# Streaming encoder layer on one core: projections opened behind the head norms, longer planned waits for chain and norms, splits behind the third quarter of value rows

## The chip, the cores and the metric

The kernel runs on one core of a Trainium2 chip. The metric is the device time of one execution in microseconds, as the median of several runs. The profile is of one further execution; times inside it count from its first instruction.

## What is computed

One layer for 576 frames (64 of a running stream, 512 of a new one) of width 1024, all in fp32. The part that the change touches is the time mixing, in 16 heads of 64, and the value rows of the gated MLP:

```python
h = rms_norm(x, g_pre_mix); p = h @ w_in            # r|k|v|lora, u, value rows, two gates
xm = p + (p_prev - p) * mu_shift                    # token shift, for r, k, v and the lora columns
kk = k * k_k; kk = kk / max(norm_per_head(kk), 1e-12)
for t: sa = S @ a_t                                 # a = -kk, b = kk * a_rate
       S = S * w_t + sa b_t^T + v_t k_t^T;  y_t = S @ r_t
o_a = (group_norm(y) + bonus) * g
o_b = u * (tril(W_s) @ layer_norm(value rows) + b)
m = sigmoid(gate_a) * (o_a @ w_proj_a) + sigmoid(gate_b) * (o_b @ w_proj_b)
x = x + rms_norm(m @ w_o);  x = x + rms_norm(swiglu(rms_norm(x)))
```

## The kernel before

Every large product is made of three fp32r matmuls (high by high, high by low, low by high part). A weight block of 128 columns is loaded by SP (`wraw`, line 295), its high part is made on ACT (`whi`, line 302) and the low part on POOL in two instructions of 512 columns (`wlo`, line 305). One such projection block (`project`) is 48 matmuls `pj` of 288 columns, two halves of the frames of 8 x 3 each.

The 16 heads are worked as 8 pairs (128 rows). The recurrence over frames is cut into chunks of 64. For each pair `elementwise` makes the decays and the head norm (matmuls `n` over the squares `q`, wait `n2`), then the chunk scores (matmuls `am` over `AR` and `BK`, wait `am0`), and signals `A`; after a bonus term it signals `elem`. `turns` transposes keys and values and signals `tb` and `values`. `inverse` inverts the chunk's triangular matrices: a recurrence of 15 steps on DVE (`Xt`, `X`, lines 862 and 865, two instructions a step), then small matmuls with copies; it signals `it`, and handles one pair after the other. `batch` (matmuls `d`, `e`, `c`, `y`) signals `inv`. `chain` carries the state over the 9 chunks: matmuls `pc` into one bank, then DVE adds `S` or `So` from that bank (line 1004); its first step has two chunks, six more follow with a planned wait `S` after each, then the output rows `py`. It starts the wait `ch0` after `inv`. `finish` makes the group norm (a POOL power `gm`, line 1035), turns the result and writes `d_oa`.

TensorE's order is written out at build time by a planner, the class `Weave`. It keeps a clock in microseconds that each matmul advances, runs the streams above as generators, and lets each go on when a planned wait (a number of the table `LAT`, with a key such as `n2@0` for pair 0 alone) or an event has passed; between them it puts the matmuls of the projection blocks, which are a queue of items. An item can be taken when its `need` event is there; `load_next` takes the first that can, two blocks ahead of its matmuls. The items are `k`, `r`, `v` of the next pair with a need, and fillers (gates and `u`, evacuated as `st`, lines 430 and 432) without one; behind the last pair come four quarters of value rows (`gv_quarter`, matmuls `gv` of 256 columns, 5 x 24 a quarter) and then the products `pa`, `pb` and so on (`behind`). A `k`, `r` or `v` block is evacuated (`shc` first, line 484) only after the pair before has signalled `elem`. Banks of PSUM are counted too: `ps1(name, hold)` books one of four for `hold` microseconds, and `clk.free(n)` waits until n are free.

The other engines' order is not written out by the planner; the framework's schedule sets it when the program is built, and each engine then works its queue in that order.

`oa_all` comes when the last pair's chain has ended: it loads the time-mix results of seven pairs, waits `oa`, and splits each into high and low part (`cut`: ACT and DVE, wait `oaj` between), loads `bias` and `wsT` after the fourth, and signals `mp`, for which `pa` waits.

Of the kernel before, what the change touches and what calls it, by code (L numbers as in the profile page):

```python
# [12 lines left out]
P = 128  # L13
# [23 lines left out]
FILL = (2, 2, 2, 2, 2, 2, 2, 6)  # L37
LAT = {
# [4 lines left out]

# [1 line left out]
}  # L45


# [186 lines left out]
def layer(tc, I, O):  # L234
# [4 lines left out]
    f = lambda t: t.bitcast(F32)  # L239

    def mk(name, **kw):
        es = ExitStack()
        return es, es.enter_context(tc.tile_pool(name=name, bufs=1, **kw))
# [18 lines left out]
    def ps1(name, hold=0.0):  # L262
        clk.take(hold)
        return psum.tile([P, 512], F32, tag="a", bufs=nb["a"], name=name)
# [5 lines left out]
    clk = Weave()  # L270

    def mmul(out, lhsT, rhs, **kw):
        n = 1
        for d in rhs.shape[1:]:
            n *= d
        rows = lhsT.shape[0]
        if rows != clk.rows:
            clk.now += 0.12
            clk.rows = rows
        if rhs.dtype == F32R:  # L280
            clk.now += 0.011 + n / 2400
        elif rows == P:
            clk.now += max(n, P) / 600
        else:
            clk.now += n / 2000 if rows == 64 else 0.037 if rows == 32 else 0.02
        return pe.matmul(out, lhsT, rhs, **kw)  # L286
# [46 lines left out]
    def mm(outs, wb, xh, xl, k, kts, halves=(0, 1), cut=HALF):  # L333

        hi, lo = wb[k // KD]
        ws = slice((k % KD) * P, (k % KD + 1) * P)
        for n, (w, x) in enumerate(((hi, xh), (hi, xl), (lo, xh))):
            for h in halves:
                mmul(outs[h], w[:, ws], x[k][:, h * cut:(cut, T)[h]], start=k == 0 and n == 0, stop=k == kts - 1 and n == 2)
# [52 lines left out]
    def item(need, srcs, body):  # L392
        return (need, lambda: [wraw(src) for src in srcs], lambda raws, pin=True: [wsplit(r, pin=pin) for r in raws], body)

    def project(blk, done, need=None, after=()):

        def body(ws):
            held = []
            for h in range(2):
                ps = psd("pj")[:, 0:HALF]  # L400
                for k in range(KD):
                    mm({h: ps}, ws, hh, hl, k, KD, halves=(h,))
                    yield
                held.append((h, ps))
                while h == 1 and any(ev not in clk.events for ev in after):
                    yield True
                while held and all(ev in clk.events for ev in after):
                    done(*held.pop(0))
        return item(need, [I["w_in"][blk]], body)

    def shift_block(name, base, p_):
        take = []

        def done(h, ps):
            if h == 0:
                take.append(Shifted(base + p_, name))
            EV[p_][name] = take[0](h, ps)
            if h == 1:
                clk.signal(name, p_)
        after = [("elem", p_ - 1)] + [("values", p_ - 1)] * (name == "v") if p_ > 0 else []  # L420
        return project(base + p_, done, need=("A", p_ - 1) if p_ > 0 else None, after=after)

    def spill(base, j, dst, need=None):
        st = []
# [72 lines left out]
    for k in range(KD):  # L497
        t = xp.tile([P, T], F32, name=f"x{k}")
# [46 lines left out]
    with tc.manual_schedule(engines={mybir.EngineType.PE}):  # L545
        pk = [psd("pk")[:, 0:HALF]]
        rb = [psd("rb"), ps1("rb")]
# [52 lines left out]
    for k in range(KD):  # L600
        t = xp.tile([P, T], F32, tag="xsq", bufs=4, name="xn")
# [15 lines left out]
    S = fixed("S", NCH + 1, HD)  # L617
# [34 lines left out]
    def elementwise(E):  # L652
        hp_ = E["hp"]
# [40 lines left out]
        for j in range(5):  # L694
            mmul(s[:, j, :], q2[:, START2[j]:START2[j] + P], bones[:, 0:P:64], start=True, stop=True)
        clk.now += LAT["n2t"]
        rn = rp.tile([P, 10], F32, tag="rn", bufs=2, name="rn")
        dve.tensor_scalar(rn, s.rearrange("p j h -> p (j h)"), 1e-24, None, ALU.max)
        dve.reciprocal(rn, rn)
# [27 lines left out]
        E["AB"] = AB  # L727
        maskb = mask.unsqueeze(1).broadcast_to([P, 4, P])
        inner = lambda pm, rows_, rows, x, c: mmul(pm[rows_].rearrange("p (a t) -> p a t", t=64), BK[rows, x, c * 64:(c + 1) * 64], AR[rows, :, c * 64:(c + 1) * 64], start=True, stop=True)
        banks = lambda: [ps1("am", 3.6).rearrange("p (j t) -> p j t", t=P) for _ in range(2)]  # L730
        yield from clk.free(4)
        pm = banks()
        for c, j, half_ in PLACES2[:8]:
# [374 lines left out]
    def keepers(xs, pair):  # L1108
        xs[0].append(pair[0])
        xs[1].append(pair[1])  # L1110

    def mixed(name, **kw):
        return R["mp"].tile([P, T], F32, tag=name, name=name, **{"bufs": 1, **kw})

    def oa_all():

        yield (("chain", NPAIR - 1), 0.0)
        r_es.close()
        R["m"], R["mp"] = mk("merge")
        raw = []  # L1120
        wide = lambda n: R["mp"].tile([P, D], F32, tag=n, bufs=1, name=n)

        def load(j):
            raw.append(wide(("bias", "wsT")[j - 2])[:, 0:T] if j in (2, 3) else mixed(("gin", "", "zb", "xt")[j // 2], bufs=2))
            sp.dma_start(raw[j], d_oa[j])

        def cut(j):
            keepers(oas, split(R["mp"], raw[j], f"m{j}", eng=(dve, pool)[OAE[j]]))

        for j in range(NPAIR - 1):  # L1130
            load(j)
        yield LAT["oa"]
        for j in range(NPAIR - 1):
            cut(j)
            if j == 3:
                R["bias"], R["wsT"] = wide("bias"), wide("wsT")
                sp.dma_start(R["bias"], I["rows"][2:3, :].broadcast_to([P, D]))
                sp.dma_start(R["wsT"].rearrange("p (g t) -> p g t", t=P), I["wsT"])
            yield LAT["oaj"]
        clk.signal("mp")  # L1140
        yield (("oa", NPAIR - 1), 0.0)
        load(NPAIR - 1)
        yield LAT["oa"]
        cut(NPAIR - 1)
        yield (("behind",), 0.0)
        r2_es.close()
        l_es.close()
        h_es.close()
        R["d0"], R["dp0"] = mk("hidden0", side="right")
        R["x"], R["xf"] = mk("xf", side="right")  # L1150
        R["f"], R["fp"] = mk("ffnin", side="right")
        R["m2"], R["map"] = mk("merge2")
        clk.signal("xf")
# [151 lines left out]
    y, xt = [], []  # L1305
# [233 lines left out]
```

## Time and profile before

| | us |
|---|---|
| median of 3 runs | 1239.83 (1239.71 to 1240.45) |
| profiled execution | 1237.7 |
| its span, first to last instruction | 1235.9 |
| of it 60 to 541.4 (pair loop): TensorE busy | 461.01 of 481.40 |
| of it 541.4 to 618.7 (value rows): TensorE busy | 73.72 of 77.30 |
| TensorE busy in all | 1187.6 |

PE is TensorE's matmuls, PEld its weight loads, DVE, ACT and POOL the vector, scalar and GpSimd engines, SP the engine that issues the DMAs. Matmuls overlap, so the step from one start to the next tells their rate and not the length of one. The granted clock stands as a share of the full 2.4 GHz.

### The profile page before, as it was taken

How to read it: one execution, taken by the hardware profiler on the slowest of the kernel's cores; microseconds unless marked ns; L12 is line 12 of the kernel's file. 1: busy time of each engine (PE TensorE's matmuls, PEld its weight loads, DVE VectorE, ACT ScalarE, POOL GpSimd, SP SyncE). 2: the span in 40 equal slices, each digit the busy share in tenths (PEclk: the TensorE clock that was granted, in tenths of full speed). 3: DMA queues.
4: the chain of work that ended last, by engine and by line, in shares of the span. 5: the costliest groups of instructions: out<-in, count | busy, mean ns of one | idle time of the engine just before them, and what ended most of it. 6: DMA issues, size and time to landing. Idle time of an engine off the chain costs nothing.

```text
span 1235.9 us, 29949 instructions
## 1 busy us (share of the span) xinstructions
PE 1187.6 (96%) x12926; PEld 1154.5 (93%) x12926; DVE 547.8 (44%) x1081; ACT 466.1 (38%) x889; POOL 614.1 (50%) x484
## 2 busy tenths in 40 slices
PE   7989999989999989899899999899999999999997
PEld 6989898889899989899899999899999999999996
DVE  5756556665555565632624431654333333300003
ACT  5555544443545434333431233442222222222220
POOL 6665354635354545333445553566565555634442
PEclk9999999998999999999999999899999999999998
DMA  5233222222222222231554542232222222252222
GB/s 184 81 106 90 72 82 85 73 70 67 72 82 85 82 63 72 79 97 63 174 173 129 181 141 86 69 128 85 74 82 86 86 86 85 69 168 83 78 77 77
DMA packets 68276, 118.05 MB, mean 96 GB/s; under 512 B 30832, under 2 KB 36208, under 8 KB 68144
## 3 DMA queue, kind: packets, MB, share of 16 engines
q1 hardware_dynamic: 68000, 116.06, 30.9%
q8 instruction: 101, 1.65, 0.6%
q14 instruction: 31, 0.25, 0.1%
q10 hardware_dynamic: 144, 0.08, 0.0%
HBM read 99.83 MB, written 16.28 MB: 94 GB/s over the span
## 4 chain that ended last, share of the span: by engine, by line
PE 76%; DVE 13%; ACT 3%; issue 3%; POOL 3%; DMA 2%; SPq 0%; DVEq 0%; POOLq 0%; ACTq 0%
PE fg L286 20%; PE pj L286 16%; PE po L286 15%; PE pb L286 4%; PE gv L286 4%; PE pa L286 3%; POOL wlo L305 2%; DVE X L865 2%; DVE Xt L862 2%; PE am L286 2%; PE z L286 1%; PE d L286 1%; DVE TD L965 1%; PE pc L286 1%; DVE y L1324 1%
## 5 line engine op out<-in xcount | busy, mean ns | idle before, releaser
L305 POOL TENSOR_TENSOR wlo<-raw,whi 128x512 fp32r<-128x512 f32 (+1 forms) x288 | 400.5, 1413 | 374.2 <-ACT whi L302 344.3
L302 ACT ACTIVATE whi<-raw 128x1024 fp32r<-128x1024 f32 x144 | 149.7, 1046 | 279.6 <-PE fg L286 174.6
L1290 DVE TENSOR_TENSOR rs<-rs,nsq 128x288 f32<-128x288 f32 (+2 forms) x12 | 9.0, 754 | 105.9 <-ACT nsq L1289 105.9
L1358 DVE TENSOR_TENSOR ft<-ft,fg 128x288 f32<-128x288 f32 x40 | 16.4, 451 | 68.0 <-PE fg L286 66.5
L1352 DVE TENSOR_TENSOR fg<-fg,rs 128x288 f32<-128x288 f32 x40 | 16.5, 453 | 63.2 <-PE fg L286 63.1
L1355 DVE SCALAR_TENSOR_TENSOR ft<-ft,fg 128x576 f32<-128x576 f32 (+1 forms) x24 | 28.7, 1197 | 19.0 <-ACT ft L1354 19.0
L1356 POOL TENSOR_TENSOR ft<-ft,rs 128x576 f32<-128x576 f32 (+1 forms) x24 | 31.8, 1327 | 7.1 <-DVE ft L1355 7.1
L286 PE MATMUL pc<-S,TD 128*128 128x64 f32 x112 | 20.9, 270 | 13.1 <-DVE So L1004 10.8
L286 PEld LDWEIGHTS pc<-S,TD 128*128 128x128 f32 x112 | 18.3, 198 | 15.6 <-DVE So L1004 12.2
L865 DVE TENSOR_TENSOR X<-X,Xt 80x15 f32<-80x15 f32 (+7 forms) x120 | 29.4, 245 | 3.9
L862 DVE TENSOR_TENSOR Xt<-X,M 80x15 f32<-80x15 f32 (+7 forms) x120 | 29.3, 245 | 3.6
L1035 POOL TENSOR_TENSOR gm<-gm,mhalf 128x10 f32<-128x10 f32 x8 | 16.2, 2022 | 27.3 <-DVE gm L1034 27.2
L1004 DVE TENSOR_TENSOR S<-pc,C 128x64 f32<-128x64 f32 x48 | 10.5, 219 | 42.8 <-PE pc L286 42.8
L286 PE MATMUL pj<-h5h,whi 128*128 128x288 f32 x88 | 28.4, 323 | 0.0
L765 POOL TENSOR_TENSOR BK<-BK,EL 128x576 f32<-128x576 f32 x16 | 19.8, 1238 | 16.9 <-PE am L286 16.9
L286 PE MATMUL pj<-h0h,whi 128*128 128x288 f32 x88 | 28.2, 320 | 0.0
L286 PE MATMUL pj<-h6h,whi 128*128 128x288 f32 x88 | 28.1, 320 | 0.0
L286 PE MATMUL pj<-h3h,whi 128*128 128x288 f32 x88 | 27.9, 317 | 0.0
L286 PE MATMUL pj<-h7h,whi 128*128 128x288 f32 x88 | 27.7, 315 | 0.0
L286 PE MATMUL pj<-h1h,whi 128*128 128x288 f32 x88 | 27.6, 314 | 0.0
L286 PE MATMUL pj<-h2h,whi 128*128 128x288 f32 x88 | 27.6, 314 | 0.0
L286 PE MATMUL pj<-h4h,whi 128*128 128x288 f32 x88 | 27.6, 313 | 0.0
(1200 smaller groups left out, 4281.4 us busy)
## 6 DMA issues: line engine op xcount, KB each, us to landing
raw<-in_w_in SPq DMA_DIRECT2D x50, 512.0 KB, 3.7
raw<-in_w_gate SPq DMA_DIRECT2D x22, 512.0 KB, 3.7
raw<-in_w_up SPq DMA_DIRECT2D x22, 512.0 KB, 3.6
raw<-in_w_down SPq DMA_DIRECT2D x16, 512.0 KB, 3.5
raw<-in_w_gv SPq DMA_DIRECT2D x8, 512.0 KB, 3.6
raw<-in_w_proj_a SPq DMA_DIRECT2D x8, 512.0 KB, 3.8
raw<-in_w_proj_b SPq DMA_DIRECT2D x8, 512.0 KB, 3.7
raw<-in_w_o SPq DMA_DIRECT2D x8, 512.0 KB, 3.7
```

The source lines that it names most:

```text
L286: return pe.matmul(out, lhsT, rhs, **kw)
L302: keep(act.activation(hi[:, :cols], raw[:, :cols], ACT.Copy))
L305: keep(pool.tensor_tensor(lo[:, c0:c1], raw[:, c0:c1], f(hi[:, c0:c1]), ALU.subtract))
L765: pool.tensor_tensor(by_chunk(BK[:, x, :]), by_chunk(BK[:, x, :]), EL[:, :, 64:65].broadcast_to([P, NCH, 64]), ALU.mult)
L862: ins = dve.tensor_tensor(t3, X[:, 0:r, s:s + 1].broadcast_to([NU, r, w]), M[:, s:s + 1, s + 1:SB].broadcast_to([NU, r, w]), ALU.mult)
L865: dve.tensor_tensor(X[:, 0:r, s + 1:SB], X[:, 0:r, s + 1:SB], t3, ALU.add)
L965: dve.tensor_tensor(TD[rows, cs, rows], ps[rows, :, 1, :], by_place[rows, cs, 0, :], ALU.add)
L1035: pool.tensor_tensor(m, m, mhalf, ALU.pow)
L1352: keep(dve.tensor_tensor(g[:, HS[h]], pg, rs2[:, HS[h]], ALU.mult))
L1355: keep(dve.scalar_tensor_tensor(t[:, ts], t[:, ts], 1.0, g[:, ts], ALU.add, ALU.mult))
L1356: pool.tensor_tensor(t[:, ts], t[:, ts], rs2[:, ts], ALU.mult)
L1358: dve.tensor_tensor(t[:, HS[h]], t[:, HS[h]], pu, ALU.mult)
```

## The change

`need` of the next pair's projections becomes a new event `n`, signalled behind the head-norm matmuls, in place of `A`. Planned waits become longer: `n2@0` 10.5 to 14.0, `ch0` 3.4 to 6.0, `S` 1.6 to 1.8, `oaj` 1.2 to 1.6; the booked time of a score bank goes from 3.6 to 4.4. The splits of `oa_all` wait in addition until `oag` (1.0) after the third quarter of value rows.

```diff
--- before.py
+++ after.py
@@ -37,11 +37,11 @@
 FILL = (2, 2, 2, 2, 2, 2, 2, 6)
 LAT = {
     "z0": 5.4, "z": 0.85, "n2": 8.2, "n2t": 0.4, "am0": 3.7, "am": 2.0, "tb0": 3.5, "tb": 1.3, "tv0": 5.2, "tv": 2.2, "bo0": 3.5, "v": 2.2, "bo": 0.4,
-    "last": 0.4, "ln": 3.5, "oa": 3.9, "oaj": 1.2, "z1": 15.0, "zs": 3.0, "zz": 1.5, "rs": 2.15, "rb": 2.8, "f": 1.1, "f0": 1.0, "sq": 0.44,
+    "last": 0.4, "ln": 3.5, "oa": 3.9, "oag": 1.0, "oaj": 1.6, "z1": 15.0, "zs": 3.0, "zz": 1.5, "rs": 2.15, "rb": 2.8, "f": 1.1, "f0": 1.0, "sq": 0.44,
     "M": 9.0, "X": 0.75, "U": 11.0, "m1": 2.3, "m2": 2.4, "mp": 4.2, "mu": 2.0, "d0": 2.2, "e0": 3.1, "y0": 3.5,
-    "ch0": 3.4, "S": 1.6, "y": 0.5, "gn1": 4.0, "gn2": 6.0, "to": 3.5, "to1": 0.45, "g": 1.8,
-
-    "am0@0": 6.4, "am0@1": 5.6, "n2@0": 10.5, "n2@1": 8.2, "tb0@1": 3.5, "M@0": 7.0,
+    "ch0": 6.0, "S": 1.8, "y": 0.5, "gn1": 4.0, "gn2": 6.0, "to": 3.5, "to1": 0.45, "g": 1.8,
+
+    "am0@0": 6.4, "am0@1": 5.6, "n2@0": 14.0, "n2@1": 8.2, "tb0@1": 3.5, "M@0": 7.0,
 }
 
 
@@ -418,7 +418,7 @@
             if h == 1:
                 clk.signal(name, p_)
         after = [("elem", p_ - 1)] + [("values", p_ - 1)] * (name == "v") if p_ > 0 else []
-        return project(base + p_, done, need=("A", p_ - 1) if p_ > 0 else None, after=after)
+        return project(base + p_, done, need=("n", p_ - 1) if p_ > 0 else None, after=after)
 
     def spill(base, j, dst, need=None):
         st = []
@@ -694,6 +694,7 @@
         for j in range(5):
             mmul(s[:, j, :], q2[:, START2[j]:START2[j] + P], bones[:, 0:P:64], start=True, stop=True)
         clk.now += LAT["n2t"]
+        clk.signal("n", hp_)
         rn = rp.tile([P, 10], F32, tag="rn", bufs=2, name="rn")
         dve.tensor_scalar(rn, s.rearrange("p j h -> p (j h)"), 1e-24, None, ALU.max)
         dve.reciprocal(rn, rn)
@@ -727,7 +728,7 @@
         E["AB"] = AB
         maskb = mask.unsqueeze(1).broadcast_to([P, 4, P])
         inner = lambda pm, rows_, rows, x, c: mmul(pm[rows_].rearrange("p (a t) -> p a t", t=64), BK[rows, x, c * 64:(c + 1) * 64], AR[rows, :, c * 64:(c + 1) * 64], start=True, stop=True)
-        banks = lambda: [ps1("am", 3.6).rearrange("p (j t) -> p j t", t=P) for _ in range(2)]
+        banks = lambda: [ps1("am", 4.4).rearrange("p (j t) -> p j t", t=P) for _ in range(2)]
         yield from clk.free(4)
         pm = banks()
         for c, j, half_ in PLACES2[:8]:
@@ -1130,6 +1131,8 @@
         for j in range(NPAIR - 1):
             load(j)
         yield LAT["oa"]
+
+        yield (("gv", 2), LAT["oag"])
         for j in range(NPAIR - 1):
             cut(j)
             if j == 3:
```

## Rows read from the trace of the kernel before

**Rows 1.** The page's sections 1 and 2, TensorE's line and the granted clock in 40 slices.

```profile
PE 1187.6 (96%) x12926; PEld 1154.5 (93%) x12926; DVE 547.8 (44%) x1081; ACT 466.1 (38%) x889; POOL 614.1 (50%) x484
...
PEclk9999999998999999999999999899999999999998
```

**Rows 2.** Busy time of each engine (with its instructions) in two stretches, the loop over the head pairs and the value rows behind it; the columns are the stretch, its length, PE, PEld, DVE, ACT and POOL busy, the granted clock, the DMA share and GB/s.

```profile
60.00:541.40 481.40, 461.01 (x7093) 437.66 (x7092) 281.46 (x658) 224.39 (x512) 229.17 (x184) 0.98 0.28 80
541.40:618.70 77.30, 73.72 (x1023) 71.05 (x1021) 33.41 (x63) 30.58 (x60) 29.81 (x21) 0.98 0.36 116
```

**Rows 3.** TensorE's waits from the start of the program to 619 us: who waited for whom, us in total, times, longest.

```profile
PE pc L286 <- DVE So L1004: 10.8, 6, 3.5
...
PE gv L286 <- POOL wlo L305: 3.3, 2, 2.7
PE n L286 <- ACT q L684: 3.1, 1, 3.1
PE pc L286 <- DVE S L1004: 2.3, 4, 1.2
PE am L286 <- ACT oo L1046: 2.2, 2, 1.4
...
PE pa L286 <- ACT s L448: 0.5, 1, 0.5
...
PE am L286 <- DVE oo L1055: 0.3, 1, 0.3
```

**Rows 4.** Busy time in five stretches that follow a wait of TensorE; columns as in rows 2, the granted clock behind POOL's.

```profile
73.41:76.82 3.41, 3.41 (x18) 3.41 (x17) 3.38 (x5) 0.00 (x0) 2.39 (x2) 0.53 0.00 0
274.80:281.62 6.82, 6.03 (x25) 6.03 (x26) 2.26 (x13) 0.00 (x0) 0.00 (x0) 0.52 0.18 41
...
462.53:465.94 3.41, 3.41 (x17) 3.21 (x16) 2.42 (x11) 2.66 (x7) 0.19 (x1) 0.53 0.64 168
523.97:527.38 3.41, 3.41 (x17) 3.41 (x17) 1.40 (x8) 0.41 (x1) 0.00 (x0) 0.53 0.13 34
602.48:605.89 3.41, 2.81 (x15) 2.41 (x14) 2.41 (x3) 0.38 (x1) 3.41 (x3) 0.53 0.39 97
```

**Rows 5.** TensorE in order of time around the head norm of pair 0: start and length in us, in brackets the idle time before and its releaser.

```profile
68.12 0.29 PE L286 MATMUL pj<-h1h,wlo 128*128 128x288 f32 x1
71.52 1.28 PE L286 MATMUL n<-cst,q 128*128 128x2 f32 x10 [3.10 <-ACT q L684]
...
73.40 0.29 PE L286 MATMUL pj<-h3h,wlo 128*128 128x288 f32 x1
73.53 0.34 PE L286 MATMUL pj<-h4h,whi 128*128 128x288 f32 x1
...
73.91 0.44 PE L286 MATMUL pj<-h4h,wlo 128*128 128x288 f32 x1
74.15 0.44 PE L286 MATMUL pj<-h5h,whi 128*128 128x288 f32 x1
```

**Rows 6.** TensorE in order of time, matmuls of the state chain: the first of pair 2, and the second steps of pairs 2, 5 and 6.

```profile
268.98 0.33 PE L286 MATMUL pc<-C,TD 128*128 128x64 f32 x2
...
275.59 0.69 PE L286 MATMUL pc<-S,TD 128*128 128x64 f32 x2 [3.53 <-DVE So L1004]
...
461.81 0.43 PE L286 MATMUL pc<-S,TD 128*128 128x64 f32 x2 [2.28 <-DVE So L1004]
...
523.59 0.43 PE L286 MATMUL pc<-S,TD 128*128 128x64 f32 x2 [2.62 <-DVE So L1004]
```

**Rows 7.** DVE in order of time, from the first to the last of the 30 recurrence instructions (`Xt`, `X`) of pair 3's inverse, with the first add of pair 2's chain; 23 of the 30 stand ahead of the add, 267.73 the first and 275.06 the last of them.

```profile
267.73 0.16 DVE L862 TENSOR_TENSOR Xt<-X,M 80x15 f32<-80x15 f32 x1
...
269.74 1.27 DVE L865 TENSOR_TENSOR X<-X,Xt 80x55 f32<-80x55 f32 x1
271.04 1.20 DVE L862 TENSOR_TENSOR Xt<-X,M 80x60 f32<-80x60 f32 x1
272.28 0.22 DVE L865 TENSOR_TENSOR X<-X,Xt 80x60 f32<-80x60 f32 x1
...
275.06 0.20 DVE L862 TENSOR_TENSOR Xt<-X,M 80x48 f32<-80x48 f32 x1
275.19 0.21 DVE L1004 TENSOR_TENSOR S<-pc,C 128x64 f32<-128x64 f32 x1
...
276.79 0.18 DVE L865 TENSOR_TENSOR X<-X,Xt 80x15 f32<-80x15 f32 x1
```

**Rows 8.** POOL in order of time, the same stretch.

```profile
269.67 2.51 POOL L305 TENSOR_TENSOR wlo<-raw,whi 128x512 fp32r<-128x512 f32 x2 [3.81 <-ACT whi L302]
```

**Rows 9.** ACT, POOL and TensorE in order of time at the start of the fourth quarter of the value rows.

```profile
598.00 1.05 ACT L302 ACTIVATE whi<-raw 128x1024 fp32r<-128x1024 f32 x1
...
598.21 2.49 POOL L1035 TENSOR_TENSOR gm<-gm,mhalf 128x10 f32<-128x10 f32 x1 [11.57 <-DVE gm L1034]
...
602.26 0.34 PE L286 MATMUL gv<-wlo,h4h 128*64 128x256 f32 x1 [2.71 <-POOL wlo L305]
```

**Rows 10.** ACT in order of time, the evacuation of the first half of a filler block (`st`) and of the `k` block behind it (`shc`).

```profile
407.67 0.41 ACT L432 ACTIVATE st<-pj 128x288 f32<-128x288 f32 x1 [1.72 <-PE pj L286]
...
417.15 0.17 ACT L484 ACTIVATE shc<-pj 128x1 f32<-128x1 f32 x1
```

**Rows 11.** TensorE in order of time, a wait of the scores `am`.

```profile
245.31 0.89 PE L286 MATMUL am<-AR,BK 64*64 64x128 f32 x24 [1.42 <-ACT oo L1046]
```

## The prediction

> **What bounds the kernel now.** I read the page first. TensorE is busy for 1187.6 us and its clock digits are 9 nearly everywhere [rows 1], so the kernel is as long as TensorE's stream of matmuls plus the holes in it. The change writes no matmul and removes none; it can only close holes, open others, or give back clock. Two stretches hold everything that it touches: the pair loop from 60 to 541.4 us, where TensorE is busy for 461.0 of 481.4 us, and the value rows with the tail of the last pair up to 618.7 us, with 73.7 of 77.3 us [rows 2].
>
> The view of TensorE's waits tells whose holes they are [rows 3]: `pc` (the state chain) waits for the DVE adds of its own step, 10.8 us for the adds that write `So` and 2.3 us for those that write `S`; `gv` waits 3.3 us for `wlo` on POOL; one head norm `n` waits 3.1 us for ScalarE's square `q`; `pa` waits 0.5 us for an evacuation; `am` waits 2.2 + 0.3 us for a bank that `oo` has still to leave. A hole is dearer than its idle time. After the long ones the granted clock is about half for a while (0.52 to 0.53 over these stretches, the lower of the two levels, 1.2 GHz) [rows 4]. I count the busy time of such a stretch times the missing share: 3.41 x 0.47 = 1.6 us behind the head norm, about 2.9 us behind 275.6 (6.03 x 0.48), 1.6 us each behind 461.8 and 523.6, and 1.3 us (2.81 x 0.47) behind the value rows' hole.
>
> **The change part by part.** *Head norm of pair 0, 10.5 to 14.0.* The last projection matmul before it starts at 68.12, the norm at 71.52 with 3.10 us idle, and behind it the matmuls come every 0.24 us instead of 0.13 us [rows 5]. The planner counts time in matmuls, so 3.5 us more is about 27 projection matmuls at 0.13 us put ahead of the norm. 3.5 covers 3.10: the hole closes with its clock, 3.1 + 1.6 = 4.7 us. What hides the 3.5 us is filler blocks, of which enough stand behind; without them it would cost 3.5 us. Next late are the scores and the inverse of pair 0, 3.5 us later in the order, with a whole pair to make it up. Bounds: 3.1 to 4.7; I take 4.7.
>
> *Chain, 3.4 to 6.0 and 1.6 to 1.8.* In the pair of rows 6 the first chain matmul starts at 268.98 and the second step waits until 275.59, 3.53 us of it idle. The DVE rows show why: the adds start at 275.19, and 23 of the 30 instructions of the next pair's recurrence (`Xt`, `X`) run between 267.73 and then [rows 7]. The adds stand in DVE's queue behind them; they don't wait for the matmul. Two of these instructions take 1.27 and 1.20 us where their neighbours take 0.22 us, and exactly then POOL runs a pair of `wlo` splits, 269.67 for 2.51 us [rows 7, 8]. The change puts the first chain matmul 2.6 us and the second step 2.8 us later, behind projections. What it gains turns on whether DVE's fixed order moves the adds along. If they stay, each of the six `So` waits shrinks by up to 2.8 us: only the first keeps 0.7 us, a gain of 10.1 us. If they move along with the matmul, they slide at most to the end of the recurrence, in that pair 1.8 us later (276.79 + 0.18 against 275.19), so that a large wait shrinks by 1.0 us; the three large ones (3.53, 2.28, 2.62 [rows 6]) give 3.0 us and the three small ones 0.2 us each: 3.6 us. No row tells which; I take the middle, 6.9 us. The four `S` waits give 0.2 us each, 0.8 us. Then no wait is much over 1.5 us, and the 1.42 us wait of `am` at 245.31 [rows 11] has none of the slow stretches of rows 4 behind it, so two of the chain's three slow stretches should go: 2.9 + 1.6 = 4.5 us. Sum 12.2 us. Bounds: 4.4 us (slow stretches stay) and 13.1 + 6.1 = 19.2 us (all goes). The chain ends 2.6 + 8 x 0.2 = 4.2 us later; behind it wait the group norm of its pair on DVE and ACT, the output rows' store on SP, and the next-but-one pair's `AR`; the planner keeps them all behind the chain's end and fills with projections, so I cost this at nothing (at most 4.2 us once, at the last pair).
>
> *Projections open behind `n` instead of `A`.* A pair takes two fillers between its `v` and the next `k`; where `A` comes just too late it takes a third, as in the pair whose third filler is evacuated at 407.67 and the next `k` at 417.15 [rows 10]. `n` always comes in time, so the third fillers (three pairs) move to the end of the loop, ahead of the value rows. Nothing is added: 48 matmuls at 0.13 us are 6.3 us each wherever they stand. The raw loads on SP, the splits on ACT and POOL and the evacuations move with them, so projections, splits and elementwise work stand elsewhere against the inverse and the chain. The latencies are still those of the old order. The nearest row for what a shifted order costs is `am` with 2.5 us of waits [rows 3]: it could lose those or gain as many. I take a loss of 2.5 us; bounds 2.5 us either way, beyond that see the rivals.
>
> *Bank hold 3.6 to 4.4.* The second pass of the scores may start 0.8 us later, 6 projection matmuls; covered, 0. Without cover 8 x 0.8 = 6.4 us.
>
> *Time-mix splits behind the third quarter.* In the last quarter's start `gv` with `wlo` waits 2.71 us at 602.26. Its split starts on ACT at 598.00, behind copies of the time-mix rows, and POOL then does a group norm's power for 2.49 us from 598.21 first [rows 9]. With the copies behind the quarter's start ACT is free for the split, and DVE of the differences. All of it: 3.3 + 0.5 + 1.3 = 5.1 us; I take 4.0 us, since the power may still be in POOL's way. Lower bound 0, and a loss of 2.7 us if the copies hold up the weights of `pa` instead. The seven splits need 1.0 + 7 x 1.6 = 12.2 us beside 120 matmuls of at most 0.13 us each, 15.6 us, so `pa` finds them ready by an estimate of 2 to 3 us; past that each us is idle. The loads of `bias` and `wsT` on SP come after the fourth split and are needed only well into `pa`.
>
> *Sum.* 4.7 + 12.2 + 4.0 - 2.5 = 18.4 us. The profiled execution (1237.7 us, span 1235.9) would come to 1219.3 us; the median of before is 2.1 us above it, so I subtract from the median: 1239.8 - 18.4 = 1221.4, forecast 1221 us.
>
> **Rivals.** *The adds move along (1229 us).* For it: the adds came late behind a queue, not for lack of PE time, and the schedule places them behind the matmul. The slow stretches stay. 4.7 + 4.4 + 4.0 - 2.5 = 10.6 us. Against: the recurrence runs out after 1.8 us more. Rows 7 and 8 show a DVE instruction held for as long as a POOL instruction, and no later chain start removes that. The Trainium skill's page "SBUF — State Buffer", section "Who interferes with whom", has it as a rule: a VectorE instruction with two SBUF inputs and a GpSimd instruction that reads SBUF lock each other out for a whole instruction. By that rule, which speaks against this part, the time would come out at this rival's 1229 us; the trace agrees with it here (1.27 and 1.20 against 0.22 us).
>
> *More splits inside the recurrence (1250 us, slower).* The chain's later start widens the stretch between the recurrence's start and the adds from 7.5 us (267.73 to 275.19) to about 10 us, and a projection block, so a pair of splits, comes about every 10 us (407.67 to 417.15 [rows 10]). If one more pair of splits falls ahead of the adds in each of the seven pairs, DVE loses 1.27 + 1.20 - 2 x 0.22 = 2.0 us each, 14.2 us, and the four small waits become long enough for the slow clock, 4 x 1.6 = 6.4 us. Against the 10.6 us of the first rival that is a loss of 10.0 us: 1249.8. It decides as soon as splits inside the recurrence cost more than five such pairs. Against: the adds would then be the last thing on DVE behind an exhausted recurrence.
>
> *Everything closes (1211 us).* 4.7 + 19.2 + 5.1 = 29.0 us, the reordering free. For it: each waiting instruction is moved by about the length of its hole (3.5 us against 3.10, 2.8 against 2.28 to 3.53 [rows 5, 6]). Against: DVE's order is not under the planner.
>
> **How the numbers follow.** Forecast 0.44, adds move along 0.24, more splits 0.20, everything closes 0.12. The range 1208 to 1248 takes in the bounds of the chain and the reordering, the clean case and the lower half of the slow one; about 0.13 stays out. A difference of 0.2% (2.5 us) is about what a measurement of this kernel can tell from none. Faster by more than that: nearly all of the forecast (0.42), most of the first rival (0.20) and the clean case (0.12): 0.74. Within: 0.10. Slower: 0.16, nearly all from the slow rival.
>
> **What would show it.** The norm of pair 0: no idle and no slow stretch at 73. The chain: the list of TensorE's waits for `So` falls from 10.8 to about 4 us; if it stays over 7, the adds moved along, and the DVE rows between the recurrence's start and `So` say how many instructions and slowed ones stand there. The fillers: two before each `k`, six before the value rows. The last quarter: its wait for `wlo` under 1 us, no new wait at `pa`. The prediction is wrong if new waits (`am`, `mp`, `v`, `pa`) exceed 6 us, or if the span of the pair loop changes for another reason than holes and clock.

## The result and the profile after

The changed kernel takes 1225.01 us (median of four runs, 1224.40 to 1228.90) against 1239.77 us for the kernel before in the same session: ratio 0.9891 [0.9866, 0.9916]. The profiled execution took 1224.4 us, its span 1222.6 us. Of all timed runs behind this document one is left out of every median as disturbed: a run of e2 below, 1881.9 us at a mean granted clock of 0.556.

The page of the kernel after, its sections 1 and 2, TensorE's line and the granted clock in 40 slices:

```profile
PE 1179.4 (96%) x12926; PEld 1145.2 (94%) x12926; DVE 524.0 (43%) x1081; ACT 466.9 (38%) x889; POOL 612.7 (50%) x484
...
PEclk9999999999999999999999999899999999999999
```

Against [rows 1], TensorE is busy for 8.2 us less and DVE for 23.8 us less, with the same count of instructions on every engine. Where that lies is seen in the busy time by stretch, the pair loop and the value rows of the kernel after (columns as in [rows 2]), then two stretches that follow the head norm and the chain wait of pair 2, and one that is new:

```profile
60.00:528.60 468.60, 452.90 (x7083) 428.49 (x7081) 261.73 (x659) 225.63 (x513) 227.20 (x184) 1.00 0.29 82
528.60:606.30 77.70, 74.02 (x1031) 71.36 (x1031) 30.74 (x66) 31.92 (x62) 30.25 (x24) 1.00 0.42 134
71.40:74.80 3.40, 3.35 (x26) 3.35 (x27) 2.52 (x4) 2.00 (x3) 2.36 (x3) 1.00 0.22 87
179.30:182.70 3.40, 3.40 (x86) 3.08 (x77) 1.85 (x4) 1.02 (x2) 1.06 (x1) 0.53 0.02 5
275.60:281.60 6.00, 5.58 (x46) 5.58 (x47) 1.65 (x8) 2.97 (x8) 4.51 (x4) 1.00 0.19 31
```

Loop and value rows together took 481.40 + 77.30 = 558.7 us in [rows 2] and take 468.60 + 77.70 = 546.3 us now, 12.4 us of the 13.3 us by which the span fell. TensorE's idle time in it went from 558.7 - 534.7 = 24.0 to 546.3 - 526.9 = 19.4 us, and its busy time, of the same 8114 to 8116 matmuls, from 534.7 to 526.9 us: 4.6 us were holes. The other 7.8 us are put down to matmuls that no longer ran at half clock. Of the five slow stretches of [rows 4], 9.0 us by the prediction's way of counting, none is left; the rows at 71.40 and 275.60 show two of the places at full clock. One slow stretch is new, at 179.30 (3.40 x 0.47 = 1.6 us). The kernel before had a sixth, which [rows 4] leave out and the prediction doesn't count, and it is gone too (again 1.6 us), so that this estimate comes to 9.0 us against the 7.8 us measured:

```profile
305.52:308.93 3.41, 3.41 (x94) 3.09 (x93) 2.45 (x4) 0.99 (x3) 1.72 (x2) 0.53 0.42 120
```

TensorE's waits in the kernel after, from 60 to 640 us (who waited for whom, us in total, times, longest):

```profile
PE pc L286 <- DVE So L1005: 8.6, 7, 1.8
PE m L286 <- DVE IT L875: 1.8, 3, 0.9
PE pa L286 <- ACT s L448: 1.7, 1, 1.7
PE gv L286 <- POOL wlo L305: 1.7, 2, 1.4
PE m L286 <- ACT whi L302: 1.6, 1, 1.6
PE z L286 <- ACT AB L936: 1.2, 1, 1.2
PE m L286 <- ACT gq L1032: 0.7, 1, 0.7
PE am L286 <- DVE AR L722: 0.6, 1, 0.6
...
PE n L286 <- ACT q L684: 0.3, 1, 0.3
```

Against [rows 3]: the wait for `q` is closed; the waits for `So` fell by 2.2 us only, but the longest from 3.5 to 1.8 us; those for `S` and `oo` are gone; waits of the inverse's matmuls and of `z`, 1.1 us before (`mp` 0.8, `m` 0.3), are 5.8 us now (the three rows of `m` and the one of `z`, and 0.5 us of `m` that are put down to issue). The view puts a wait down to what ended last; `m` reads only `IT` and `AB`, so its waits for `whi` and `gq` need another reading, which is given at e9. Why `So` kept most of its wait is seen on DVE in order of time, the recurrence of pair 3 and the first adds of pair 2's chain, the same place as [rows 7]:

```profile
268.35 0.16 DVE L863 TENSOR_TENSOR Xt<-X,M 80x15 f32<-80x15 f32 x1
...
275.53 0.18 DVE L866 TENSOR_TENSOR X<-X,Xt 80x15 f32<-80x15 f32 x1
275.62 0.21 DVE L1005 TENSOR_TENSOR S<-pc,C 128x64 f32<-128x64 f32 x1
275.75 0.21 DVE L1005 TENSOR_TENSOR So<-pc,C 128x64 f32<-128x64 f32 x1
```

All 30 instructions of the recurrence now stand ahead of the adds, in this pair (23 before) and in the six others (12 to 21 before). The adds moved along, up to the recurrence's end and no further. But here none of the 30 is a long one: the longest of them takes 0.22 us. Counting DVE's rows over the eight pairs, a pair of `wlo` splits fell inside five recurrences before (two instructions of some 1.2 us each, as in [rows 7]) and inside one now (in another a single instruction is lengthened).

### The profile page after: what moved, and what is told of

It reads as the page before. It is cut to its first block, busy times and chain, and to the rows that moved or that the text cites. A ratio compares the mean times of both kernels' runs of the same rounds, so it can differ in the third digit from the quotient of the medians.

```text
span 1222.6 us, 29930 instructions
## 1 busy us (share of the span) xinstructions
PE 1179.4 (96%) x12926; PEld 1145.2 (94%) x12926; DVE 524.0 (43%) x1081; ACT 466.9 (38%) x889; POOL 612.7 (50%) x484
## 4 chain that ended last, share of the span: by engine, by line
PE 75%; DVE 14%; ACT 3%; DMA 3%; issue 3%; POOL 2%; SPq 0%; DVEq 0%; ACTq 0%; POOLq 0%
PE fg L286 21%; PE po L286 15%; PE pj L286 15%; PE pb L286 4%; PE pa L286 3%; PE gv L286 3%; DVE Xt L863 2%; DVE X L866 2%; PE am L286 1%; PE z L286 1%; PE m L286 1%; POOL wlo L305 1%; PE pc L286 1%; PE wv L286 1%; PE d L286 1%
## 5 line engine op out<-in xcount | busy, mean ns | idle before, releaser
L688 POOL TENSOR_TENSOR aq<-aq,k 128x576 f32<-128x576 f32 x8 | 11.4, 1421 | 34.4 <-PE pc L286 30.0
L863 DVE TENSOR_TENSOR Xt<-X,M 80x15 f32<-80x15 f32 (+7 forms) x120 | 25.8, 215 | 4.8 <-DMA M<-d_inv 1.2
L866 DVE TENSOR_TENSOR X<-X,Xt 80x15 f32<-80x15 f32 (+7 forms) x120 | 25.2, 210 | 4.1
L286 PE MATMUL pj<-h0h,wlo 128*128 128x288 f32 x88 | 26.3, 299 | 0.2 <-POOL wlo L305 0.2
```

The source lines that it names most:

```text
L688: pool.tensor_tensor(aq, aq, k, ALU.mult)
L863: ins = dve.tensor_tensor(t3, X[:, 0:r, s:s + 1].broadcast_to([NU, r, w]), M[:, s:s + 1, s + 1:SB].broadcast_to([NU, r, w]), ALU.mult)
L866: dve.tensor_tensor(X[:, 0:r, s + 1:SB], X[:, 0:r, s + 1:SB], t3, ALU.add)
```

## The experiments

Twelve kernels, each timed beside the kernel before. The table gives the stretch from the first `z` matmul to the first `pa` matmul by the busy time in that stretch: its length, TensorE's idle time (length less busy), its busy time, and DVE's. Two counts of DVE's rows follow, which the end of this section uses: in how many of six pairs both `AR` products of a pair stand ahead of both products that the group norm of the pair two before it makes on `Y`, and how many of the 240 recurrence instructions take over 1 us. Everything from the length on is read from one profiled execution, whose time can lie off the median (e1 1246.2, e2 1243.7, e7 1235.0, e12 1222.5 us). Edits are shown shortened; `...` and comments stand for what is left out.

| kernel | median us | ratio to before, 95% | length | idle | TensorE busy | DVE busy | `AR` first | over 1 us |
|---|---|---|---|---|---|---|---|---|
| before | 1239.8 | | 556.5 | 24.2 | 532.3 | 313.3 | 0 | 10 |
| after | 1225.0 | 0.9891 [0.9866, 0.9916] | 544.2 | 19.6 | 524.6 | 290.6 | 6 | 2 |
| e1 before + norm | 1250.8 | 1.0103 [1.0076, 1.0129] | 572.8 | 33.1 | 539.7 | 316.4 | 0 | 10 |
| e2 before + chain | 1250.5 | 1.0109 [1.0076, 1.0141] | 570.0 | 34.8 | 535.2 | 310.4 | 0 | 14 |
| e3 before + reorder | 1261.1 | 1.0178 [1.0148, 1.0208] | 582.2 | 40.4 | 541.8 | 309.6 | 0 | 12 |
| e4 before + splits | 1238.0 | 1.0001 [0.9982, 1.0021] | 559.3 | 24.2 | 535.1 | 313.1 | 0 | 10 |
| e5 after, reorder undone | 1237.5 | 1.0002 [0.9974, 1.0030] | 553.6 | 22.8 | 530.8 | 310.3 | 0 | 8 |
| e6 after, chain undone | 1265.3 | 1.0237 [1.0192, 1.0282] | 584.3 | 48.5 | 535.9 | 320.7 | 0 | 12 |
| e7 after, norm undone | 1229.4 | 0.9944 [0.9918, 0.9970] | 553.8 | 22.5 | 531.3 | 300.6 | 6 | 10 |
| e8 before + reorder + chain | 1249.3 | 1.0103 [1.0058, 1.0148] | 568.6 | 35.0 | 533.6 | 314.1 | 2 | 14 |
| e9 e8, group norm held back | 1259.1 | 1.0167 [1.0134, 1.0201] | 577.7 | 37.3 | 540.4 | 306.4 | 4 | 11 |
| e10 after, order pinned | 1236.8 | 0.9990 [0.9974, 1.0006] | 557.4 | 28.0 | 529.4 | 314.2 | 6 | 34 |
| e11 after, `ch0` 8.0 | 1235.5 | 0.9970 [0.9949, 0.9992] | 553.6 | 24.3 | 529.3 | 301.9 | 6 | 12 |
| e12 after, hold undone | 1228.4 | 0.9922 [0.9898, 0.9947] | 547.4 | 21.3 | 526.1 | 306.2 | 6 | 6 |

### One part alone

The prediction's theory is that the parts are terms of a sum, each priced at its own hole. The rival is that a part moves work on the other engines too, so that its worth depends on the others.

**e1, the norm alone.**

```diff
-    "am0@0": 6.4, "am0@1": 5.6, "n2@0": 10.5, "n2@1": 8.2, ...
+    "am0@0": 6.4, "am0@1": 5.6, "n2@0": 14.0, "n2@1": 8.2, ...
```

> The kernel before with the head norm of pair 0 at 14.0 alone. Theory (holes close where the waiting matmuls are moved): the 3.1 us hole and the slow stretch behind it go, 1239.8 - 4.5 = 1235 us, the rest of the trace as before. Rival (the hole passes to the next late step, the scores or the inverse of pair 0): within 1.5 us of before, with a new wait of 2 to 3 us between 72 and 135 us.

1250.8 us, 1.0% slower, outside both expectations. TensorE's waits in e1, 60 to 640 us:

```profile
PE pc L286 <- DVE So L1004: 14.2, 5, 3.0
PE am L286 <- DVE oo L1055: 3.1, 2, 1.6
...
PE z L286 <- ACT ta L666: 2.5, 1, 2.5
...
PE n L286 <- ACT q L684: 0.4, 1, 0.4
```

The hole was closed, 3.1 to 0.4 us, as priced; and waits in pairs that the edit doesn't name took its place. One number that is read for pair 0 alone changed waits far behind it.

**e2, the chain alone.**

```diff
-    "ch0": 3.4, "S": 1.6, ...
+    "ch0": 6.0, "S": 1.8, ...
```

> The kernel before with the chain's two waits (6.0 and 1.8) alone. Theory A (DVE's order moves the adds along to the end of the recurrence, which caps the wait): all 30 recurrence instructions stand ahead of the first adds, the waits for So still sum to 8 to 10 us, none over 2.8 us, and with them go two or three of the chain's slow clock stretches: 1239.8 - 7 = 1233 us. Theory B (what matters is that splits on POOL no longer fall into the recurrence, which only the projections' new order does): recurrence instructions of 1.2 us stay in four pairs, the waits stay over 2.3 us in three pairs and so does the slow clock: 1238 to 1240 us.

1250.5 us, 1.1% slower, outside both expectations, and where the prediction's slow rival had said 1249.8. What that rival described is there to be seen. DVE in order of time in e2, the recurrence of pair 3 and the first adds of pair 2's chain:

```profile
271.04 0.16 DVE L862 TENSOR_TENSOR Xt<-X,M 80x15 f32<-80x15 f32 x1
...
274.31 1.22 DVE L862 TENSOR_TENSOR Xt<-X,M 80x64 f32<-80x64 f32 x1
275.56 1.20 DVE L865 TENSOR_TENSOR X<-X,Xt 80x64 f32<-80x64 f32 x1
...
281.10 0.21 DVE L1004 TENSOR_TENSOR S<-pc,C 128x64 f32<-128x64 f32 x1
```

POOL in the same stretch of e2:

```profile
274.17 2.51 POOL L305 TENSOR_TENSOR wlo<-raw,whi 128x512 fp32r<-128x512 f32 x2 [9.96 <-ACT whi L302]
```

The adds stand behind all 30 instructions, as in the kernel after, but a split pair lies inside the recurrence, in seven of the eight pairs. The rival's number came out partly by chance, though: five pairs had such splits before, so two are new and not seven, and the waits for `So` rose by 3.5 us only (10.8 to 14.3) while the 2.3 us for `S` went. The rest are waits that it didn't name, the two largest of them by TensorE's waits in e2:

```profile
PE z L286 <- ACT ta L666: 5.1, 1, 5.1
PE to L290 <- DVE AB L742: 4.3, 4, 1.1
```

**e3, the reordering alone.**

```diff
-    need=("A", p_ - 1) if p_ > 0 else None
+    need=("n", p_ - 1) if p_ > 0 else None
+    clk.signal("n", hp_)        # behind the head-norm matmuls
```

> The kernel before with the projections opened behind the head norms alone. Theory A: the third fillers leave three pairs and nothing is gained by itself, the chain's waits stay near 11 us with their slow stretches: 1238 to 1243 us. Theory B: the 1.2 us recurrence instructions go in most pairs, the waits for So shrink by about 2 us in each of those and the slow stretches go: 1239.8 - 8 = 1232 us.

1261.1 us, 1.8% slower, outside both expectations and the worst of the parts. TensorE's waits in e3, the second and third largest (`So` has 13.5 us):

```profile
PE am L286 <- DVE AR L722: 8.4, 2, 4.3
PE m L286 <- DVE IT L875: 5.1, 1, 5.1
```

The 4.3 us, on DVE in order of time in e3:

```profile
368.75 2.94 DVE L1038 TENSOR_TENSOR Y<-Y,gm 128x640 f32<-128x640 f32 x1 [1.38 <-POOL gm L1036]
371.61 1.81 DVE L722 TENSOR_TENSOR AR<-r,EL 128x576 f32<-128x576 f32 x1
```

The product `AR`, for which the scores `am` of its pair wait, is queued behind the second product of the group norm. That one first waits 1.38 us for POOL's power and then takes 2.94 us, where the same product of the same pair takes 0.82 us at its place in the kernel after.

**e4, the splits alone.**

```diff
+    "oag": 1.0, "oaj": 1.6        # before: "oaj": 1.2
+    yield (("gv", 2), LAT["oag"])
```

> The kernel before with the time-mix splits behind the third quarter alone. Theory: the 2.7 us wait for the low weight part and its slow stretch shrink to about 1.4 us without slow stretch, but the first matmul of the next product waits 1 to 2 us, as in the changed kernel: 1239.8 - 2 = 1238 us. Rival (the tail of the last pair is what collides, and needs the fillers moved in front of the value rows): the wait stays over 2 us, no difference.

1238.0 us, no difference, as the rival had it. The waits are those of before, `gv` for `wlo` among them (3.0 us in two, the longest 2.7).

So no part alone is worth a gain; three of the four made the stretch of the table 13 to 26 us longer in the profiled executions, whatever became of the hole at which they were read.

### One part taken out

**e5, the reordering undone.**

```diff
-    need=("n", p_ - 1) if p_ > 0 else None
+    need=("A", p_ - 1) if p_ > 0 else None
```

> The changed kernel with the projections' need put back to A. Theory (what gains is DVE's queue: both AR products of pair p+2 ahead of both group-norm products of pair p in every pair; in this kernel's queue a group-norm product stands between or ahead of them in every pair): the gain is lost, 1240 to 1252 us, as with the chain's waits alone. Rival (the wait lengths do it, the need is a bystander): 1222 to 1228 us.

**e6, the chain undone** (`ch0` 3.4, `S` 1.6).

```diff
-    "ch0": 6.0, "S": 1.8, ...
+    "ch0": 3.4, "S": 1.6, ...
```

> The changed kernel with the chain's waits put back to 3.4 and 1.6. Theory (DVE's queue; here one group-norm product stands between the two AR products in every pair, and the first adds stand inside the recurrence): the gain is lost, 1238 to 1255 us, with waits of am for AR. Rival (the need and the head norm do it): 1222 to 1230 us.

**e7, the norm undone.**

```diff
-    "n2@0": 14.0
+    "n2@0": 10.5
```

> The changed kernel with pair 0's head norm put back to 10.5. Theory (DVE's queue keeps AR ahead of the group norm in every pair here): only the hole at 68 us and its slow clock come back, 1225 + 4.7 = 1230 us. Rival (the head norm's 3.5 us set the phase of the whole loop, without them it falls back as each part alone did): 1240 us or more.

**e8, reordering and chain on the kernel before** (the edits of e2 and e3).

```diff
+    "ch0": 6.0, "S": 1.8        # before: 3.4, 1.6
+    need=("n", p_ - 1), clk.signal("n", hp_)
```

> The kernel before with need and chain waits together, nothing else. Theory (DVE's queue; here a group-norm product stands between the two AR products in five of seven pairs): no gain, 1238 to 1250 us. Rival (need and chain are the two parts that must come together, head norm and bank hold are small): 1230 us.

Without the reordering the gain is gone (1237.5); without the longer chain waits the kernel is 2.4% slower than before (1265.3); without the norm 1229.4 us, 4.4 us above the changed kernel by the medians of two sessions, 0.5% by the ratios. The lost gain that the theory expected of e5, e6 and e8 came, in its range only in e8: e5 lies 2.5 us under it, e6 10 us above, with waits of `m` and not of `am`. The 1230 us that it expected of e7 came too. The reordering that costs 1.8% alone is thus worth 12.5 us in the company of the others. And reordering with chain alone is slower (1249.3), so these two are needed and don't suffice: e7 differs from e8 by the longer bank hold and the splits alone, and is 20 us faster. The splits wait for the third quarter of value rows, so in the pair loop e7 differs from e8 by the bank hold alone; yet its first `gv` matmul starts at 544.2 us and that of e8 at 556.4 us, 12.2 of the 14.0 us between the two profiled executions. Without the norm the hold, which the prediction took for nothing, thus makes most of the difference; with the norm (e12 below) it is worth little.

The theory I took from these runs is the order on DVE: who stands first there, the group norm's second product (which waits for POOL) or the products and copies that TensorE waits for next. DVE in order of time in the kernel after, behind pair 2's chain:

```profile
293.08 2.01 DVE L722 TENSOR_TENSOR AR<-r,EL 128x576 f32<-128x576 f32 x1
...
296.16 0.83 DVE L875 STREAM_TRANSPOSE IT<-IV 128x640 f32<-128x640 f32 x1
...
298.25 1.28 DVE L743 TENSOR_TENSOR AB<-am,rmul 128x512 f32<-128x512 f32 x2
...
303.19 1.87 DVE L1038 TENSOR_TENSOR Y<-Y,gm 128x640 f32<-128x640 f32 x1 [2.07 <-POOL gm L1036]
```

Three of them in e6, behind the chain of another pair:

```profile
375.85 1.77 DVE L1038 TENSOR_TENSOR Y<-Y,gm 128x640 f32<-128x640 f32 x1 [2.90 <-POOL gm L1036]
377.55 1.28 DVE L743 TENSOR_TENSOR AB<-am,rmul 128x512 f32<-128x512 f32 x2
...
379.54 0.83 DVE L875 STREAM_TRANSPOSE IT<-IV 128x640 f32<-128x640 f32 x1
```

And TensorE's waits in e6, the largest, with the matmul that waited at this place:

```profile
PE m L286 <- DVE IT L875: 26.4, 7, 6.2
...
380.51 0.68 PE L286 MATMUL m<-IT,AB 16*32 16x16 f32 x37 [6.23 <-DVE IT L875]
```

In the kernel after, DVE's 2.07 us of waiting for POOL's power come behind `IT` and the scores' copies; in e6 the 2.90 us come ahead of them, and TensorE stands still for 6.23 us. That order accounts for the largest waits of e6 and e3; the next three runs were to show whether it is the cause of the whole.

### The order made or broken by itself

**e9, the order of the group norm forced on e8.** Its planned start waits until the `AR` products of the next pair but one are issued.

```diff
+            clk.signal("ar", hp_)              # behind AR's product
+        if hp_ + 2 < NPAIR:
+            yield (("ar", hp_ + 2), 0.0)       # ahead of the group norm
```

> The kernel before with need and chain waits, and one thing more: the group norm of pair p is planned only behind the AR products of pair p+2. No other wait changes. Its DVE queue has both AR products ahead of both group-norm products in four of six pairs, where need and chain alone had one. Theory (that order is what gains): most of the loss of need and chain alone goes, 1249 to about 1236 us, and the waits of the inverse's small matmuls for the turned tile (6.0 us) and for AB (4.3 us) fall under 4 us together. Rival (the order is a companion of the gain, not its cause): 1245 to 1252 us.

1259.1 us, slower than e8 and than both expectations. The products stood ahead of the group norm's in four of the six pairs. TensorE's waits in e9, the largest:

```profile
PE m L286 <- ACT gq L1035: 14.8, 5, 3.2
```

Five waits of `m` are new, put down to ACT's `gq`. One of them ends at 366.47; on DVE ahead of it in e9:

```profile
361.95 2.88 DVE L777 SCALAR_TENSOR_TENSOR q<-r,vec,ta 128x576 f32<-128x576 f32 x1
364.76 0.81 DVE L1033 TENSOR_TENSOR Y<-Y,gm 128x640 f32<-128x640 f32 x1
365.49 0.83 DVE L876 STREAM_TRANSPOSE IT<-IV 128x640 f32<-128x640 f32 x1
```

`IT`, which `m` reads, ends at 366.32, and `gq`, which it doesn't read, 0.02 us later (365.61 + 0.73). `m` starts 0.15 us behind `IT`'s end, as it does in e6, where `IT` is the one named (379.54 + 0.83 = 380.37, start 380.51). So these waits are most likely `IT`'s, and so is the kernel after's for `whi`: there `IT` ends at 178.81, `m` starts at 178.96.

```profile
177.98 0.83 DVE L875 STREAM_TRANSPOSE IT<-IV 128x640 f32<-128x640 f32 x1
```

In e9 `IT` is late behind a product `q` that takes 2.88 us while POOL works on `rmul` (361.50, 2.72 us), and 0.80 us at its shortest in the same run. The order was mended in four pairs and the time went to another neighbour on DVE. That this one order brings the gain by itself is not borne out.

**e10, the changed kernel with the recurrence and the chain's adds kept in the order in which the code issues them.**

```diff
-            if s == 0:
-                tc.keep_in_program_order(ins)
-            dve.tensor_tensor(X[...], X[...], t3, ALU.add)
+            tc.keep_in_program_order(ins)
+            tc.keep_in_program_order(dve.tensor_tensor(X[...], X[...], t3, ALU.add))
...
+                tc.keep_in_program_order(dve.tensor_tensor(dst, pc[:, i], add(c), ALU.add))
```

> The changed kernel with DVE's recurrence instructions and chain adds kept in the order in which the planner writes them: the first adds then stand behind 5 to 7 of the 15 recurrence steps, not behind all 15. TensorE's order is the same. Theory (the adds' place in DVE's queue is all that the chain's second step waits for): the waits for So fall from 8.6 us to under 2 us, 1225 - 7 = 1218 us. Rival (the recurrence, delayed by the adds, makes the next inverse late, or the queue shifts elsewhere): no gain, new waits of the small matmuls m.

**e11, the changed kernel with a still later chain.**

```diff
-    "ch0": 6.0
+    "ch0": 8.0
```

> The changed kernel with the chain's first wait at 8.0 in place of 6.0. Theory (the recurrence's end caps the wait, the adds already stand behind all of it): the waits for So, at most 1.8 us each, fall to under 1 us in all, 1225 - 7 = 1218 us. Rival (the chain, 2 us later again, disturbs the order of scores and group norm): 1228 us or more.

Neither gained, as both rivals had it: 1236.8 and 1235.5 us, most of the changed kernel's gain lost. The largest wait in each, e10 first:

```profile
PE pc L286 <- DVE S L1004: 16.7, 13, 3.3
```

```profile
PE pc L286 <- DVE So L1005: 8.4, 2, 6.2
```

In e10 the adds stand between the steps of the recurrence, which now lasts 13.6 to 23.0 us in the first seven pairs instead of 7.4 to 9.4, with four to seven long instructions in six of them. In e11 five of the seven `So` waits are gone, which is what the later start was for, and one of 6.2 us is there. DVE ahead of it in e11:

```profile
460.62 2.32 DVE L866 TENSOR_TENSOR X<-X,Xt 80x28 f32<-80x28 f32 x1
...
464.07 1.20 DVE L866 TENSOR_TENSOR X<-X,Xt 80x15 f32<-80x15 f32 x1
465.19 0.21 DVE L1005 TENSOR_TENSOR S<-pc,C 128x64 f32<-128x64 f32 x1
```

POOL in the same stretch of e11:

```profile
460.58 2.33 POOL L702 TENSOR_TENSOR rmul<-cst,rn 128x1280 f32<-128x1280 f32 x1 [3.23 <-DVE rn L700]
...
463.97 2.49 POOL L305 TENSOR_TENSOR wlo<-raw,whi 128x512 fp32r<-128x512 f32 x2
```

Three POOL instructions run one behind the other (an `AR` product stands between these two) beside the last three instructions of the recurrence, and each of the three takes 1.06 to 2.32 us instead of about 0.2 us.

**e12, the bank hold undone.**

```diff
-        banks = lambda: [ps1("am", 4.4)...
+        banks = lambda: [ps1("am", 3.6)...
```

> The changed kernel with the score banks booked for 3.6 again. Theory (DVE's queue keeps its order of scores and group norm in every pair without it): 1224 to 1228 us, no difference. Rival (the bank's 0.8 us set the phase of the splits against the recurrence): 1235 us or more, and recurrence instructions of 1.2 us in four pairs or more.

1228.4 us (1222.48 to 1230.66, against 1224.40 to 1228.90): the ranges overlap, the hold is worth 3.4 us by the medians of two sessions and may be worth nothing here. None of the twelve is clearly faster than the changed kernel.

**Two counts over all traces.** The last two columns of the table put the runs side by side. Both `AR` products stand ahead of the group norm in all six pairs in five kernels only: the changed one, e12, e7, e11 and e10, and these have the five lowest ratios. Among them the ratio rises with the number of recurrence instructions over 1 us: 2, 6, 10, 12 and 34 of them go with 0.9891, 0.9922, 0.9944, 0.9970 and 0.9990. Without the order no such row forms: 8 to 14 of them go with anything from 1.0000 (the kernel before) to 1.0237. So the two together rank the kernels that gain (for e10, whose interval takes in 1, no gain is shown), and neither does alone. This is a ranking of single profiled executions found afterwards, and no run set either count by itself.

## Why the prediction was right, and where it wasn't

The time was right: 1221 us forecast, 1225 us measured, a gain of 18.4 us foreseen and 14.8 us found (12 to 13 us against the medians of before in the later sessions, 1237.1 to 1237.9 us). Its terms, in the whole change:

- **Norm**, 4.7 us: the idle time went from 3.10 to 0.31 us and the slow stretch behind it is gone, 2.8 + 1.6 = 4.4 us; taking the norm out (e7) costs 4.4 us by the medians, though e7 also has five recurrences with splits inside instead of one, so that the two numbers need not be the same thing. The assumption that filler blocks hide the 3.5 us held in this company and failed alone (e1, 13.4 us slower than the runs of before beside it).
- **Chain**, 12.2 us: `So` gave 2.2 us (6.9 foreseen), `S` 2.3 (0.8), the slow stretches 2.9 + 1.6 + 1.6 = 6.1 (4.5): 10.6 us. By the prediction's own sign (`So` over 7 us, and it is 8.6) the first rival had the adds right: they moved along to the recurrence's end. It was wrong in that the slow stretches would stay: no wait for `So` is over 1.8 us now and none of them has a slow stretch behind it. That they are so short goes with the one recurrence with splits inside instead of five, which neither the forecast nor the rival had worked out.
- **Reordering and bank hold**, a loss of 2.5 and nothing: `am` gained 2.5 us (no wait for `oo`) and lost 0.6 us for `AR`; `m`, `mp` and `z` went from 1.1 to 5.8 us, and the slow stretch at 179.30 costs 3.40 x 0.47 = 1.6 us. Together -2.5 + 0.6 + 4.7 + 1.6, a loss of 4.4 us, past the bound of 2.5 us. That these waits belong to this part and not to another is how I book them; no run shows it. The fillers came as foreseen, two before each `k` and six before the value rows.
- **Splits**, 4.0 us: `gv` and `pa` went from 3.3 + 0.5 us and 1.3 us of clock to 1.7 + 1.7 us, a gain of 1.7 us. The rows of the last quarter now show `wlo` at 588.28 right behind its high part, with the power out of the way, as foreseen; but `gv` still waits for it, 1.4 us at the longest, and `pa` waits 1.2 us more than before, so both signs given for this part failed (under 1 us, no new wait). The step that failed is that ACT would be free: it still makes copies of time-mix rows (the last at 586.58) right ahead of that high part (587.16).

4.4 + 10.6 - 4.4 + 1.7 = 12.3 us, against the 12.4 us that the two stretches gave. That it comes out says little: holes and clock are all that the stretch can lose, however they are booked, and the sixth slow stretch, a term that the prediction left out, would add 1.6 us. (The chain has seven waits `S` and not eight, so its end was to come 4.0 us later and not 4.2; the sum doesn't use it.)

What failed is a step that all the terms share: "The planner keeps them all behind the chain's end" and "covered, 0", that is, a part whose own hole closes costs nothing elsewhere while TensorE has fillers. Three of the four parts alone cost 13.2 to 23.7 us against the 1237.4 us of before beside them, much of it in waits for DVE and ACT that no term names, and the reordering, bounded at 2.5 us either way by the nearest row, cost 23.7 us alone and brought 12.5 us in the whole. The planner covers a wait in TensorE's order only; DVE, ACT and POOL have their queues from the framework's schedule, and the runs show these queues in another order after each part. That the sum came out near was luck in this sense: the whole falls on a good order, and nothing in the profile of before that the prediction used showed that it would. The chance of 0.20 for the slow rival was, seen from the twelve runs, not too high: three of four single parts and three of the other eight kernels are over 1% slower.

The Trainium skill's rule that I weighed, "SBUF — State Buffer", section "Who interferes with whom", agrees with the slowed rows shown here: 1.22 and 1.20 against 0.22 us in e2, 2.32 us beside a POOL instruction of 2.33 us in e11. It did not lead to the first rival's time as I had it, for I took it that a split keeps its place inside the recurrence, and the whole change moved the splits out of all but one.

What stays open is which property of the order makes the difference. Shown is that the gain is gone without the reordering and without the chain's waits, that these two alone don't bring it, and that the difference lies in idle and half-clock time of TensorE. DVE's order of group norm and scores accounts for the largest waits of e3 and e6, but it is not enough: e10 and e11 keep it in all six pairs and lose most of the gain. DVE's busy time falls in the kernel after (290.6) but e12 has 306.2 us and is nearly as fast. That where POOL's instructions fall against DVE's queue is the common cause is argued from the rows of e2, e3, e9 and e11 and from the two counts; a kernel with the splits off POOL, which would have shown it, was not tried.

## What to carry to other kernels

When only one engine's order is planned by hand and the others' queues follow from a schedule, price a change of the plan as one new order and not as a sum of holes: here three parts cost 1.0 to 1.8% each alone and the whole gains 1.1%. Before a planned wait is lengthened, list what the other engines have queued between the old place and the new, and look for the instruction there that waits for a slow engine or is slowed beside it. Measure the whole and each part left out; a part measured alone says little about its worth in company.

## What the hardware showed beside that

TensorE, in order of time in the kernel after, around the new slow stretch:

```profile
178.96 0.98 PE L286 MATMUL m<-IT,AB 16*32 16x16 f32 x80 [1.58 <-ACT whi L302]
```

A wait of 1.58 us, followed by 80 matmuls of 16 columns without a gap, has 3.4 us at a granted clock of 0.53 behind it (the row at 179.30 above), while the chain's wait of 1.77 us at 276.02, followed by a chain step and projections, has none. So the length of a wait alone did not decide. Nor did the kind of matmul behind it: a wait of 2.13 us ahead of the same 80 matmuls in e8 (494.93) has no slow stretch behind it, and of two chain waits of 1.74 us the one in e7 (518.11) has one and the one in the kernel after (508.27) has none. The sixth slow stretch of the kernel before, at 305.52, follows no wait over 0.34 us:

```profile
303.57 0.85 PE L286 MATMUL m<-IT,AB 16*32 16x16 f32 x80 [0.34 <-DVE IT L874]
```

What decides is open here. A price of 1.6 us of clock for a wait of 1.5 to 3 us is therefore a chance and not a certainty.

The kernel before is less steady than its first three runs said (1239.71 to 1240.45): beside the experiments it ran from 1228.9 to 1241.1 us in 59 runs, so that three runs could not have settled a difference of 0.2%, as the prediction had it.
